# One transformer block with 32 experts on one core: a fixed TensorE order around the router, a split first gather, later norm vectors, and padded weight places

## The chip, the core and the metric

The kernel runs on one core of a Trainium2 chip. The core has five engines with a queue each: TensorE (PE; its weight loads are shown apart as PEld), VectorE (DVE), ScalarE (ACT), GpSimd (POOL) and SyncE (SP), which here issues nearly all DMAs. Each queue is worked in order, and engines wait for each other by semaphores. 16 DMA engines move data between HBM and SBUF; TensorE writes to PSUM. The metric is the device time of one execution in microseconds (us); the median of the runs is compared.

## The reference, cut to what matters

256 tokens of width 1024 go through one block. The mixer (three kinds of attention and state space branches) ends in a projection; its sum with the residual is normalised; a router picks 4 of 32 experts per token; the experts' outputs are added with softmaxed gates; a second normalisation follows.

```python
mix = merged @ w_o
h = layer_norm(ALPHA * h + mix, ln1_g, ln1_b)
logits = h @ w_router + b_router                    # [256, 32]
top_val, top_idx = top_k(logits, 4); gate = softmax(top_val)
for e in range(32):                                  # tokens that chose e
    g, lin = split(x_e @ w_gate_up[e] + b_gate_up[e])    # w_gate_up[e]: 1024 x 2048
    act = min(g, 7) * sigmoid(1.702 * min(g, 7)) * (clip(lin, -7, 7) + 1)
    ffn[tokens of e] += gate * (act @ w_down[e] + b_down[e])
out = layer_norm(ALPHA * h + ffn, ln2_g, ln2_b)
```

All of it is in float32; the experts' weights are 32 x 12 MiB.

## The kernel before

**Tiles.** The 256 tokens are two tiles t of 128 rows; `h` holds both. The width 1024 is 8 pieces k of 128 for products, and two halves n of 512 for PSUM banks.

**The weight stream.** `chunk` (L74) issues one DMA of 1 MiB, 128 rows of 8 KB, on SP's queue into a slot of 8 KB a partition. There are 24 such slots under four tags (13 u, 3 w, 4 s, 4 z); a pattern hands them out in turn, and other big tiles take their turns in the same slots: the halves of `w_o`, `xT1` (the transposed tokens for the router), `r` (what is left of `h` after a rounding to bf16) and `l1s` (the first norm's scale and shift, spread over the partitions). An expert has 12 chunks, 8 of `w_gate_up` and 4 of `w_down`, loaded in the order gate_up of expert e, then down of expert e - 1. SP's queue is in order: a chunk that waits until its slot has been read holds up all behind it. Around the router, the chunks that are due wait in turn for project (L208), the router's logits, expert 0's first reads (`pl` L1094), and the slot of `r`. The slots lie behind the small tiles of pool `cp`, from byte 7136 of each partition on, which is 480 past a multiple of 512 and 224 past one of 256.

**Around the router.** `project(t, n, k)` adds the product with piece k of `w_o` to a PSUM bank by three matmuls (L206 to L208). `half(t, n)` adds that bank to `h` (DVE L924), transposes four blocks of it (PE L927), copies them to `xT1` (ACT L928), takes statistics, and multiplies by the router's weights (PE L933, the logits). `route(t)` ends the norm without its scale and shift (`rs`, `nmr` on DVE, then ACT L948 on `h`), marks the four greatest logits (`selb`, DVE L953), counts the rank of each token in its expert's list (PE L956 and L957; called rank here) and writes `posm`, the places (DVE L959).

**Expert 0.** `sel` picks the expert's row of the biases (GpSimd). One-hot matrices `oh` (DVE L1046) gather the tokens' rows of both tiles from `h` by 16 matmuls of float32 (PE L1060), 8 pieces by 2 tiles, accumulating in PSUM; DVE and ACT put the norm's scale and shift on and write `xT`. `then`, which is `residual` for expert 0, splits `h` into three bf16 terms for later gathers, then spreads the norm's vectors by `spread` (PE L144, four groups of 4 matmuls into tile `pc`), copies them to `l1s` (ACT L1004) and applies them to `acc`, which is `h` (DVE L1008 and L1009). `pw` transposes the places with gates for the later scatter (L1083). The bias matmuls come next, then `up` (L1094): for each k a pair of matmuls to `pg` and one to `pl`, each pair reading one chunk. Experts from 1 on gather from the bf16 terms.

**What sets the order.** The program is traced into a scheduler that simulates a timeline and orders each engine's queue by it; `tc.issue_after(x)` fixes that what is traced inside comes after x. Tiles' readers and writers get their semaphores from the same pass.

Of the kernel before, what the change touches and what calls it, by code (L numbers as in the profile page):

```python
# [56 lines left out]
def block_kernel(ctx: ExitStack, tc: tile.TileContext, a: dict, out: bass.AP):  # L57
# [44 lines left out]
    G.memset(one, 1.0)  # L102
    lg = [cp.tile([128, NE + 4], F32, name=f"lg{t}") for t in range(NT)]
# [78 lines left out]
    with ExitStack() as fx:  # L182
# [735 lines left out]
        raw, stats = [], [f2.tile([128, 2, 6], F32, tag="bs", name="bs") for t in range(NT)]  # L918

        def half(t, n):  # L920


            zh = h[:, t, n * 512:(n + 1) * 512]
            V.scalar_tensor_tensor(zh, pz[t][n], 0.5 / ALPHA, zh, op0=OP.mult, op1=OP.add)  # L924
            p = bank("mm" if t else "tr")
            for k in range(4):
                PE.transpose(p[:, k * 128:(k + 1) * 128], zh[:, k * 128:(k + 1) * 128], ident)  # L927
            S.activation(xT1[:, 4 * n:4 * n + 4, t * 128:(t + 1) * 128], p.rearrange("p (k c) -> p k c", k=4), AF.Copy)  # L928
            V.bn_stats(stats[t][:, n, :], zh)
            if n == 0:  # L930
                raw.append(bank("sc", 3))
            for k in range(4 * n, 4 * n + 4):
                PE.matmul(raw[t][:, :NE], xT1[:, k, t * 128:(t + 1) * 128], wr[:, k, :], start=k == 0, stop=k == KT - 1)  # L933

        def route(t):
# [6 lines left out]
            lgt = lg[t][:, :NE]  # L942
            V.scalar_tensor_tensor(lgt, swr, nmr[:, 0:1], raw[t][:, :NE], op0=OP.mult, op1=OP.add)
            V.scalar_tensor_tensor(lgt, lgt, rs, brt, op0=OP.mult, op1=OP.add)
            tt(nmr[:, 1:2], nmr[:, 0:1], rs, OP.mult)
            for n in range(2):
                zh = h[:, t, n * 512:(n + 1) * 512]
                S.activation(zh, zh, AF.Identity, scale=rs, bias=nmr[:, 1:2])  # L948

# [3 lines left out]
            V.tensor_scalar(selb[:, t, :], mark[:, :NE], 3e38, None, op0=OP.is_equal)  # L953
            p = bank("mm" if t else "tr")
            for tp in range(t):
                PE.matmul(p[:, :NE], onesb, selb[:, tp, :], start=tp == 0, stop=False)  # L956
            PE.matmul(p[:, :NE], before, selb[:, t, :], start=t == 0, stop=True)  # L957

            V.scalar_tensor_tensor(posm[:, t, :], selb[:, t, :], -1e6, p[:, :NE], op0=OP.mult, op1=OP.add)  # L959

        for k in range(2, KT):
            project(1, 0, k)
        for n in range(2):
            half(0, n)
        route(0)
        for k in range(2, 5):
            project(1, 1, k)
        half(1, 0)
        for k in range(5, KT):
            project(1, 1, k)  # L970
        half(1, 1)
        route(1)
# [16 lines left out]
    def residual(x):  # L989
# [43 lines left out]
    def expert(mp, pm, gu, dn, pick_e, pos_e, gate_e, slots, then=None, last=None, after=None, first=False):  # L1033
# [6 lines left out]
        if first:  # L1040
            oh = mp.tile([128, 512], F32, tag="aT", name="oh", bufs=1)[:, :NT * CAP].rearrange("p (t c) -> p t c", t=NT)
        else:
            oh = mp.tile([128, NT, CAP], BF, tag="oh", name="oh")
        og = mp.tile([128, NT, 128], F32, tag="og", name="og", bufs=1)
        for t in range(NT):
            end = V.tensor_scalar(oh[:, t, :], slots[:, :CAP], pos_e(t), None, op0=OP.is_equal)  # L1046
        if first:
            with tc.issue_after(end.ins):
                gates(mp)
        for t in range(NT):  # L1050
            V.tensor_scalar(og[:, t, :], slots, pos_e(t), gate_e(t), op0=OP.is_equal, op1=OP.mult)
        xT = mp.tile([128, KT, CAP], F32, tag="xT", name="xT")
        xg = pm.tile([128, KT, CAP], F32, tag="xg", name="xg", bufs=1)
        if first:

            xg1 = pm.tile([128, 512], F32, tag="pc", name="xg", bufs=2)[:, :256].rearrange("p (k c) -> p k c", k=4)
            for k in range(KT):
                o = xg[:, k, :] if k < 4 else xg1[:, k - 4, :]
                for t in range(NT):
                    after = PE.matmul(o, h[:, t, k * 128:(k + 1) * 128], oh[:, t, :], start=t == 0, stop=t == 1)  # L1060
            wide_l = lambda i: lc[:, i, 0:4, None].to_broadcast([128, 4, CAP])
            tt(xT[:, 0:4], xg[:, 0:4], wide_l(0), OP.mult)
            tt(xT[:, 0:4], xT[:, 0:4], wide_l(1), OP.add)
            for k in range(4, KT):
                S.activation(xT[:, k, :], xg1[:, k - 4, :], AF.Identity, scale=lc[:, 0, k:k + 1], bias=lc[:, 1, k:k + 1])
        else:
            for k in range(KT):
                n = 0
                for b in range(3):
                    for t in range(NT):  # L1070
                        PE.matmul(xg[:, k, :], hb[t][b][:, k * 128:(k + 1) * 128], oh[:, t, :], start=n == 0,  # L1071
                                  stop=n == 5)
                        n += 1
            tt(xT, xg, lc[:, 0, :, None].to_broadcast([128, KT, CAP]), OP.mult)
            gg(xT, xT, lc[:, 1, :, None].to_broadcast([128, KT, CAP]), OP.add)

        if then:
            with tc.issue_after(after.ins):
                then(xT[:, KT - 1, 0:1])

        pw = pm.tile([128, 512], F32, tag="pt", name="pw", bufs=1)
        for t in range(NT):
            PE.transpose(pw[:, t * 128:(t + 1) * 128], og[:, t, :], ident)  # L1083
        ohT = mp.tile([128, 256], F32R, tag="ohT", name="ohT", bufs=3)
        gs = mp.tile([128, 1], F32, tag="gs", name="gs", bufs=3)
        V.tensor_scalar(ohT, pw[:, :256], 0.0, None, op0=OP.is_gt)
        V.tensor_reduce(gs, pw[:, :256], axis=AX.X, op=OP.max)

# [9 lines left out]
        with tc.issue_after(after.ins) if after else ExitStack():  # L1098
            up(pg, 0, sel, bias, True, False)
            up(pl, DFF, sel, bias, True, False)  # L1100
        for k in range(KT):
# [70 lines left out]
    for e in range(NE):  # L1172
# [3 lines left out]
        if e == NE - 1:  # L1176
            weights(e, KT, 12)
            l2 = big("l2", [128, 2, 2, 512])
            for i in range(4):
# [5 lines left out]
                      residual if e == 0 else further_blocks if e == 1 else None, last, after, e == 0)  # L1185
# [161 lines left out]
```

## Time and profile before

| | |
|---|---|
| median of 3 runs | 1289.65 us (1288.69 to 1295.11) |
| the profiled execution's own time | 1292.44 us |
| its span | 1290.7 us |
| mean granted TensorE clock | 0.985 |
| busy: PE, PEld, DVE, ACT, POOL | 1225.6, 623.2, 579.6, 285.6, 55.7 us |
| moved by DMA | 451.95 MB |

The span is the time from the first to the last instruction of the profiled execution. The page cuts it into 40 slices of 32.3 us. [...] In the views, `<-` in an operation stands between what is written and what is read; behind a row's duration, a bracket tells how long the engine had been idle and what ended it. Where rows are grouped (x8), the duration is that of the group.

### The profile page before, as it was taken

The page shows a single profiled execution, that of the slowest core. Times are in us where ns is not written, and L with a number is a line of the kernel's source. Part 1 is how long each engine was busy: PE and PEld are TensorE (multiplying, and loading weights), DVE is VectorE, ACT ScalarE, POOL GpSimd, SP SyncE. Part 2 cuts the span into 40 slices and gives each one's busy share as a digit, 9 for nine tenths or more (in the row PEclk, how much of TensorE's full clock was granted, in tenths as well). Part 3 has the DMA queues.
Part 4 walks back from the last instruction along what each step waited for, and adds up shares of the span by engine and source line. Part 5 has one row for each costly group of instructions (what it writes and reads, how often), then busy time and mean ns, then how long its engine had stood idle before and what let it go on. Part 6 is the DMA issues. An engine that isn't in the chain of part 4 may idle for free. (4 is left out here: it accounts for less than half of the span.)

```text
span 1290.7 us, 17685 instructions
## 1 busy us (share of the span) xinstructions
PE 1225.6 (95%) x7261; PEld 623.2 (48%) x7262; DVE 579.6 (45%) x1170; ACT 285.6 (22%) x514; POOL 55.7 (4%) x104
## 2 busy tenths in 40 slices
PE   7999999999999999999999999999999989999994
PEld 6657898789634434444444443333333333333331
DVE  6699975667633423334333343333333333333225
ACT  4245659863311000000100000010000000000111
POOL 1000000000000000000000000000000000000000
PEclk9999989999799999999999999999999999999998
DMA  7344447357799999999999999999999999999993
GB/s 273 105 137 183 169 147 224 133 189 305 284 420 418 420 419 419 419 420 419 419 418 420 418 419 419 420 420 418 420 419 419 420 418 420 420 419 420 419 419 120
DMA packets 65333, 451.95 MB, mean 350 GB/s; under 512 B 8896, under 2 KB 9056, under 8 KB 11360
## 3 DMA queue, kind: packets, MB, share of 16 engines
q1 hardware_dynamic: 64960, 450.26, 86.2%
q8 instruction: 58, 0.95, 0.3%
q10 hardware_dynamic: 288, 0.52, 0.1%
q14 instruction: 27, 0.22, 0.0%
HBM read 449.70 MB, written 1.05 MB: 349 GB/s over the span
## 5 line engine op out<-in xcount | busy, mean ns | idle before, releaser
L1094 PE MATMUL pg<-w,xT 128*64 128x512 f32 x1024 | 292.8, 608 | 13.0 <-DMA w<-in_w_gate_up 11.4
L1094 PE MATMUL pl<-w,xT 128*64 128x512 f32 x1024 | 285.8, 593 | 0.0
L1141 PE MATMUL py<-w,aT 128*64 128x512 f32 x1024 | 241.7, 599 | 18.5 <-DMA w<-in_w_down 17.7
L78 DVE TENSOR_TENSOR h<-h,pc 128x512 f32<-128x512 f32 x128 | 82.2, 684 | 294.9 <-PE pc L1156 294.9
L1094 PEld LDWEIGHTS pl<-w,xT 128*64 128x64 f32 x1024 | 95.0, 137 | 127.9 <-issue 104.7
L1141 PEld LDWEIGHTS py<-w,aT 128*64 128x64 f32 x1024 | 69.5, 136 | 158.7 <-issue 95.1
L1114 ACT ACTIVATE sg<-gc 128x512 f32<-128x512 f32 x32 | 20.1, 630 | 564.4 <-DVE gc L1113 564.4
L1094 PEld LDWEIGHTS pg<-w,xT 128*64 128x64 f32 x1024 | 74.7, 136 | 132.0 <-DMA w<-in_w_gate_up 67.5
L1148 DVE SCALAR_TENSOR_TENSOR ys<-py,gs,ys 128x512 fp32r<-128x512 f32 x64 | 48.0, 751 | 169.4 <-ACT ys L1147 166.3
L1147 ACT ACTIVATE ys<-py,gs 128x512 fp32r<-128x512 f32 x64 | 44.0, 688 | 253.5 <-PE py L1141 238.0
L1156 PE MATMUL pc<-ys,ohT 128*128 128x512 f32 x256 | 77.0, 422 | 0.9 <-DVE h L78 0.8
L1156 PEld LDWEIGHTS pc<-ys,ohT 128*128 128x128 f32 x256 | 42.9, 188 | 57.9 <-issue 50.7
L194 DVE TENSOR_TENSOR hl<-w,hl 128x1024 fp32r<-128x1024 f32 x48 | 58.2, 1221 | 14.9 <-ACT hl L193 14.7
L81 POOL TENSOR_TENSOR xT<-xT,lc 128x512 f32<-128x512 f32 x31 | 39.8, 1284 | 525.6 <-DVE xT L78 525.6
L208 PE MATMUL mm<-hTh,hl 128*128 128x256 f32 x192 | 57.1, 298 | 2.0 <-DVE hl L194 2.0
L1071 PEld LDWEIGHTS <-hb 128*128 128x128 bf16 x1240 | 45.0, 98 | 27.5 <-issue 26.7
L206 PE MATMUL mm<-hTh,hl 128*128 128x256 f32 x192 | 57.4, 299 | 0.0
L207 PE MATMUL mm<-hTl,hl 128*128 128x256 f32 x192 | 56.4, 294 | 0.0
L193 ACT ACTIVATE hl<-w 128x1024 fp32r<-128x1024 f32 x48 | 50.0, 1054 | 26.6 <-DMA w<-in_w_g 13.9
L1113 DVE TENSOR_SCALAR gc<-pg 128x512 f32<-128x512 f32 x32 | 22.1, 692 | 71.1 <-PE pg L1094 71.1
L1071 PE MATMUL xg<-oh,hb 128*128 128x64 bf16 x1240 | 49.7, 193 | 0.0
L1071 PE MATMUL xg<-oh,bias 128*128 128x64 bf16 x248 | 44.2, 193 | 0.0
(390 smaller groups left out, 1454.0 us busy)
## 6 DMA issues: line engine op xcount, KB each, us to landing
w<-in_w_gate_up SPq DMA_DIRECT2D x256, 1024.0 KB, 19.9
w<-in_w_down SPq DMA_DIRECT2D x128, 1024.0 KB, 19.9
w<-in_w_g SPq DMA_DIRECT2D x12, 1024.0 KB, 4.9
w<-in_w_s_glu SPq DMA_DIRECT2D x4, 1024.0 KB
w<-in_w_o SPq DMA_DIRECT2D x4, 1024.0 KB, 4.8
w<-in_w_memk SPq DMA_DIRECT2D x2, 1024.0 KB, 10.2
w<-in_w_u SPq DMA_DIRECT2D x2, 1024.0 KB, 8.6
w<-in_w_memv SPq DMA_DIRECT2D x2, 1024.0 KB, 5.2
```

What stands on the lines that cost most here:

```text
L78: V.tensor_tensor(o, x, y, op=op)
L193: S.activation(hi, src, AF.Copy)
L194: (eng or V).tensor_tensor(lo, src, hi.bitcast(F32), op=OP.subtract)
L206: PE.matmul(o, lhsT(0), rhs(0), start=start, stop=False)
L207: PE.matmul(o, lhsT(0), rhs(1), start=False, stop=False)
L208: PE.matmul(o, lhsT(1), rhs(0), start=False, stop=stop)
L1071: PE.matmul(xg[:, k, :], hb[t][b][:, k * 128:(k + 1) * 128], oh[:, t, :], start=n == 0, stop=n == 5)
L1094: m = PE.matmul(p_[hf * 64:(hf + 1) * 64, :], lhsT, w[:, o + hf * 512:o + (hf + 1) * 512], start=start, stop=stop)
L1141: end = PE.matmul(py[j * 64:(j + 1) * 64, :], a4[:, k // 4, k % 4 + j, :], dn(k + j, hf), start=k + j == 1, stop=k == 6)
L1147: S.activation(y2[:, 0], py, AF.Copy, scale=gs)
L1148: V.scalar_tensor_tensor(y2[:, 1], py, gs, y2[:, 0].bitcast(F32), op0=OP.mult, op1=OP.subtract)
L1156: PE.matmul(pc, ohT[:, t * 128:(t + 1) * 128], ys[hf][:, i], start=i == 0, stop=i == 1)
```

## The change

Five things are changed.

1. TensorE's order around the router is written out: a function `step` puts each piece after the piece before by `issue_after`. `half` and `route` are split into `residual_half`, `turn` (transposes), `logits`, `norm`, `four` and `rank`.
2. The first expert's gather is split by tile. Tile 0's 8 pieces are gathered as soon as tile 0's places are known, into a bank of their own (`xg0`), and ACT writes them with scale and shift to `x0`. Tile 1's 8 pieces follow later, and DVE scales them and adds `x0`. Expert 0's bias matmuls come before the gather of tile 1, the places' transposes after its second k.
3. `l1s` and its ACT copies are gone; `start_sum` lets DVE read the spread vectors from PSUM, and it runs in expert 1 behind k = 3 and k = 5.
4. `l1s` no longer takes a slot from the weights.
5. A pad of 32 bytes a partition in pool `cp` moves the slots from byte 7136 to 7168, a multiple of 512.

```diff
@@ pool cp
+    cp.tile([128, 8], F32, name="pad")
...
@@ around the router
+        def step(f, *args):
+            with tc.issue_after(done[0].ins) if done[0] else ExitStack():
+                done[0] = f(*args) or done[0]
...
-        for k in range(2, KT):
-            project(1, 0, k)
-        for n in range(2):
-            half(0, n)
-        route(0)
-        for k in range(2, 5):
-            project(1, 1, k)
-        half(1, 0)
-        for k in range(5, KT):
-            project(1, 1, k)
-        half(1, 1)
-        route(1)
+        some(0, range(2, KT - 1))
+        done[0] = project(1, 0, KT - 1)
+        for n in range(2):
+            residual_half(0, n)
+            step(turn, 0, n)
+        residual_half(1, 0)
+        step(some, 1, range(2, 5))
+        step(turn, 1, 0)
+        raw = [bank("sc", 3) for t in range(NT)]
+        step(logits, 0)
+        n0 = norm(0)
+        four(0, *n0)
+        step(some, 1, range(5, KT))
+        residual_half(1, 1)
+        step(rank, 0)
+
+        oh0 = fp.tile([128, CAP], F32)
+        V.tensor_scalar(oh0, slot[:, :CAP], posm[:, 0, 0:1], None, op0=OP.is_equal)
+        step(turn, 1, 1)
+        n1 = norm(1)
+        xg0 = bank("av", 1).rearrange("p (k c) -> p k c", c=CAP)
+        step(gather, xg0, h[:, 0, :], oh0, range(0, 2))
+        step(logits, 1)
+        four(1, *n1)
+        step(gather, xg0, h[:, 0, :], oh0, range(2, KT))
+        x0 = hb2.bitcast(F32).rearrange("p (k c) -> p k c", c=CAP)
+        for k in range(KT):
+            S.activation(x0[:, k, :], xg0[:, k, :], AF.Identity, scale=lc[:, 0, k:k + 1], bias=lc[:, 1, k:k + 1])
+        step(rank, 1)
+        ranked = done[0]
@@ residual, for expert 0
-        l1s = big("l1s", [128, 4, 512], **at("l1s"))
-        for i in range(4):
-            S.activation(l1s[:, i], spread(gb1, i, pm.tile([128, 512], F32, tag="pc", name="pc", bufs=2)), AF.Copy)
-        for i in range(2):
-            for t in range(NT):
-                at_ = acc[:, t, i * 512:(i + 1) * 512]
-                V.scalar_tensor_tensor(at_, at_, ALPHA, l1s[:, i], op0=OP.mult, op1=OP.mult)
-                V.scalar_tensor_tensor(at_, l1s[:, 2 + i], ALPHA, at_, op0=OP.mult, op1=OP.add)
+    def start_sum(i):
+
+        g_, b_ = (spread(gb1, 2 * j + i, pm.tile([128, 512], F32, tag="pc", name="pc", bufs=2)) for j in range(2))
+        for t in range(NT):
+            at_ = acc[:, t, i * 512:(i + 1) * 512]
+            V.scalar_tensor_tensor(at_, at_, ALPHA, g_, op0=OP.mult, op1=OP.mult)
+            V.scalar_tensor_tensor(at_, b_, ALPHA, at_, op0=OP.mult, op1=OP.add)
@@ expert
+        if first:
+
+            oh = mp.tile([128, 512], F32, tag="aT", name="oh", bufs=1)[:, :CAP]
+            end = V.tensor_scalar(oh, slots[:, :CAP], pos_e(1), None, op0=OP.is_equal)
+            with tc.issue_after(end.ins):
+                gates(mp)
+            xg1 = pm.tile([128, 512], F32, tag="pc", name="xg", bufs=2).rearrange("p (k c) -> p k c", c=CAP)
+
+            with tc.issue_after(ranked.ins):
+                end = biases()
+            with tc.issue_after(end.ins):
+                for k in range(KT):
+                    PE.matmul((xg, xg1)[k // 4][:, k, :], h[:, 1, k * 128:(k + 1) * 128], oh, start=True, stop=True)
+            for i, p_ in enumerate((xg, xg1)):
+                sl = slice(4 * i, 4 * i + 4)
+                tt(xT[:, sl], p_[:, sl], wide_l(0)[:, sl], OP.mult)
+                tt(xT[:, sl], xT[:, sl], x0[:, sl], OP.add)
...
+            if first and k == 1:
+                with tc.issue_after(end.ins):
+                    places()
...
-                      residual if e == 0 else further_blocks if e == 1 else None, last, after, e == 0)
+                      residual if e == 0 else further_blocks if e == 1 else None,
+                      start_sum if e == 1 else last, after, e == 0)
```

TensorE's queue between project and the router, before. `av` is the bank of tile 1's second half, `hl` the pieces of `w_o` (`hl_2873` is k = 5, `hl_2902` k = 6, `hl_2905` k = 7), `tr` and `mm` the banks of the transposes of tile 0 and 1, `sc` the logits.

```order
L207 MATMUL av_2691<-hl_2873,mgTh_2672 128x512
L208 MATMUL av_2691<-hl_2873,mgTl_2673 128x512
L206 MATMUL av_2691<-hl_2902,mgTh_2672 128x512
L927 MATMUL tr_2942<-ident_61,h_180 128x128 x4
L927 MATMUL tr_2955<-ident_61,h_180 128x128 x4
L207 MATMUL av_2691<-hl_2902,mgTh_2672 128x512
L208 MATMUL av_2691<-hl_2902,mgTl_2673 128x512
L206 MATMUL av_2691<-hl_2905,mgTh_2672 128x512
L207 MATMUL av_2691<-hl_2905,mgTh_2672 128x512
L208 MATMUL av_2691<-hl_2905,mgTl_2673 128x512
L927 MATMUL mm_3005<-ident_61,h_180 128x128 x4
L933 MATMUL sc_2949<-s_w_router_421,xT1_2867 128x32 x8
```

And the same stretch after; here `hl_2848`, `hl_2851` and `hl_2871` are k = 2 to 4, `hl_2874` is k = 5.

```order
L209 MATMUL av_2692<-hl_2848,mgTl_2674 128x512
L207 MATMUL av_2692<-hl_2851,mgTh_2673 128x512
L208 MATMUL av_2692<-hl_2851,mgTh_2673 128x512
L209 MATMUL av_2692<-hl_2851,mgTl_2674 128x512
L207 MATMUL av_2692<-hl_2871,mgTh_2673 128x512
L208 MATMUL av_2692<-hl_2871,mgTh_2673 128x512
L209 MATMUL av_2692<-hl_2871,mgTl_2674 128x512
L938 MATMUL mm_2969<-ident_61,h_181 128x128 x4
L945 MATMUL sc_2975<-s_w_router_422,xT1_2868 128x32 x8
L207 MATMUL av_2692<-hl_2874,mgTh_2673 128x512
L208 MATMUL av_2692<-hl_2874,mgTh_2673 128x512
L209 MATMUL av_2692<-hl_2874,mgTl_2674 128x512
```

Before, k = 5 of project stands ahead of all transposes and logits. After, the transposes of tile 0 (in the two rows ahead of these), those of tile 1's first half and tile 0's logits stand ahead of k = 5.

TensorE's queue at the start of expert 0, before. `xg` are the gathered rows, `pc` the spread vectors, `pw` the places, `w_1621` the first chunk.

```order
L1060 MATMUL xg_3106<-oh_3084,h_180 128x64
L1060 MATMUL xg_3107<-oh_3084,h_180 128x64
L1060 MATMUL xg_3106<-oh_3084,h_180 128x64 x7
L1060 MATMUL xg_3107<-oh_3084,h_180 128x64 x7
L144 MATMUL pc_3142<-gbin_ln1_g_2676,ident_61 128x128 x4
L1083 MATMUL pw_3174<-ident_61,og_3085 128x128 x2
L1094 LDWEIGHTS sel_3082
L1094 MATMUL pg_3181<-bias_441,sel_3082 64x512
L1094 LDWEIGHTS sel_3082
L1094 MATMUL pg_3181<-bias_441,sel_3082 64x512
L1094 LDWEIGHTS sel_3082
L1094 MATMUL pl_3182<-bias_441,sel_3082 64x512
```

And after, from the end of rank(1) on; `w_1622` is the same chunk.

```order
L976 LDWEIGHTS before_2687
L976 MATMUL mm_3084<-selb_2921,before_2687 128x32
L1097 LDWEIGHTS sel_3102
L1097 MATMUL pg_3107<-bias_442,sel_3102 64x512
L1097 LDWEIGHTS sel_3102
L1097 MATMUL pg_3107<-bias_442,sel_3102 64x512
L1097 LDWEIGHTS sel_3102
L1097 MATMUL pl_3108<-bias_442,sel_3102 64x512
L1097 LDWEIGHTS sel_3102
L1097 MATMUL pl_3108<-bias_442,sel_3102 64x512
L1117 MATMUL xg_3106<-oh_3109,h_181 128x64 x4
L1117 MATMUL xg_3126<-oh_3109,h_181 128x64 x4
```

The gather is half as long here, the bias matmuls stand ahead of it, and the spread and the places are no longer between gather and up.

SP's queue of weight chunks, with the waits, before: the first rows are those that wait for project, the row with `Activation_49` waits for the logits (`xT1`'s slot), the next for expert 0's first k, the one with `DVE_49` for `r`'s slot.

```order
L74 DMA w<-in_w_gate_up 128x2048 [waits DMAHW7_49,PE_49]
L74 DMA w<-in_w_gate_up 128x2048 [waits PE_49]
L74 DMA w<-in_w_gate_up 128x2048 [waits DMAHW1_49,PE_49]
L74 DMA w<-in_w_gate_up 128x2048 [waits DMAHW2_49]
L74 DMA w<-in_w_down 128x2048 [waits DMAHW3_49]
L74 DMA w<-in_w_down 128x2048 [waits DMAHW4_49,PE_49,Activation_49]
L74 DMA w<-in_w_gate_up 128x2048 [waits DMAHW5_49,PE_49]
L74 DMA w<-in_w_down 128x2048 [waits DMAHW6_49,DVE_49]
```

And after.

```order
L74 DMA w<-in_w_gate_up 128x2048 [waits DMAHW7_49,PE_49]
L74 DMA w<-in_w_gate_up 128x2048 [waits PE_49]
L74 DMA w<-in_w_gate_up 128x2048 [waits DMAHW1_49,PE_49]
L74 DMA w<-in_w_gate_up 128x2048 [waits DMAHW2_49]
L74 DMA w<-in_w_down 128x2048 [waits DMAHW3_49]
L74 DMA w<-in_w_down 128x2048 [waits DMAHW4_49]
L74 DMA w<-in_w_down 128x2048 [waits DMAHW5_49,PE_49,Activation_49]
L74 DMA w<-in_w_gate_up 128x2048 [waits DMAHW6_49,PE_49]
L74 DMA w<-in_w_gate_up 128x2048 [waits DMAHW7_49,PE_49]
L74 DMA w<-in_w_down 128x2048 [waits DMAHW0_49,DVE_49]
```

One chunk of `w_down` more, which waits for an earlier DMA alone, stands ahead of the row that waits for expert 0's first k, and the chunk behind that waits for its second k.

## Rows read from the trace of the kernel before

**Rows 1.** The page's slices: what the DMA engines moved, GB/s in 40 equal slices.

```profile
GB/s 273 105 137 183 169 147 224 133 189 305 284 420 418 420 419 419 419 420 419 419 418 420 418 419 419 420 420 418 420 419 419 420 418 420 420 419 420 419 419 120
```

**Rows 2.** Long window: us; busy PE, PEld, DVE, ACT, POOL; PEclk, DMA share, GB/s.

```profile
600.00:800.00 200.00, 198.12 (x1186) 85.86 (x1184) 70.87 (x125) 18.73 (x29) 11.14 (x14) 1.00 1.01 419
```

**Rows 3.** Waits of the whole span: total us, times, longest us.

```profile
PEld pg L1094 <- DMA w<-in_w_gate_up: 67.5, 69, 2.6
```

**Rows 4.** Windows of 2 us around the router; columns as in group 2.

```profile
324.00:326.00 2.00, 2.00 (x13) 1.67 (x12) 1.86 (x11) 0.00 (x0) 0.00 (x0) 1.00 0.36 147
326.00:328.00 2.00, 2.00 (x15) 1.74 (x14) 0.80 (x4) 1.85 (x4) 0.00 (x0) 1.00 0.70 193
...
334.00:336.00 2.00, 1.61 (x8) 1.64 (x8) 2.00 (x17) 0.53 (x2) 0.63 (x3) 0.50 0.99 418
...
342.00:344.00 2.00, 2.00 (x9) 1.44 (x9) 0.15 (x1) 1.78 (x4) 0.00 (x0) 0.50 0.23 94
344.00:346.00 2.00, 2.00 (x9) 0.87 (x10) 1.89 (x5) 1.67 (x3) 0.00 (x0) 0.50 0.00 0
346.00:348.00 2.00, 2.00 (x8) 0.51 (x6) 2.00 (x3) 1.38 (x2) 0.00 (x0) 0.75 0.00 0
348.00:350.00 2.00, 2.00 (x10) 0.82 (x7) 2.00 (x4) 0.73 (x1) 0.00 (x0) 1.00 0.43 115
...
352.00:354.00 2.00, 2.00 (x15) 1.02 (x15) 1.21 (x3) 0.60 (x1) 0.00 (x0) 1.00 0.81 270
```

**Rows 5.** SP's queue: issues (start us, us), and its waits in 323:333 and 345:357.

```profile
325.47 3.30 SPq L74 DMA_DIRECT2D w<-in_w_gate_up  x4
...
347.86 0.33 SPq L74 DMA_DIRECT2D w<-in_w_gate_up  x1
351.14 0.33 SPq L74 DMA_DIRECT2D w<-in_w_down  x1
...
SPq L74 <- PE av L208: 12.8, 2, 10.9
...
SPq L74 <- PE pl L1094: 19.2, 3, 15.3
```

**Rows 6.** TensorE's timeline, router to first up: start us, us, idle before.

```profile
325.51 1.03 PE L927 MATMUL tr<-ident,h 128*128 128x128 f32 x8
326.30 0.48 PE L207 MATMUL av<-hl,mgTh 128*128 128x512 f32 x1
...
327.54 0.60 PE L927 MATMUL mm<-ident,h 128*128 128x128 f32 x4
327.97 1.87 PE L933 MATMUL sc<-s_w_router,xT 128*128 128x32 f32 x16
329.68 0.63 PE L927 MATMUL mm<-ident,h 128*128 128x128 f32 x4
...
333.44 0.18 PE L957 MATMUL mm<-selb,before 128*128 128x32 bf16 x1 [1.32 <-DVE selb L953]
334.39 7.06 PE L1060 MATMUL xg<-oh,h 128*128 128x64 f32 x32 [0.76 <-DVE oh L1046]
341.38 2.07 PE L144 MATMUL pc<-gbin_ln_g,ident 16*128 16x128 f32 x8
...
344.00 0.64 PE L1094 MATMUL pg<-bias,sel 128*64 128x512 bf16 x2
...
344.86 1.92 PE L1094 MATMUL pg<-w,xT 128*64 128x512 f32 x4
```

**Rows 7.** ScalarE's and DVE's timeline: scaling of gathered rows, a norm vector's use.

```profile
341.49 1.29 ACT L1065 ACTIVATE xT<-xg,lc 128x64 f32<-128x64 f32 x4 [6.37 <-PE xg L1060]
...
351.28 1.29 DVE L1008 SCALAR_TENSOR_TENSOR h<-h,l1s 128x512 f32<-128x512 f32 x2 [0.16 <-ACT l1s L1004]
```

**Rows 8.** DMA packets, MB, share of 16 engines, in 15.17:15.27 and 21.94:21.97.

```profile
q1 hardware_dynamic: 92, 0.00, 58.6%
...
q1 hardware_dynamic: 13, 0.00, 29.4%
```

More of the change, by code (lines that the diff above doesn't have):

```diff
@@ L1038, in expert @@
         G.tensor_copy(sel, pick_e.to_broadcast([128, CAP]))
[L1040 to L1043, printed above, removed]
         og = mp.tile([128, NT, 128], F32, tag="og", name="og", bufs=1)
[L1045 to L1049, printed above, removed]
@@ L1050, in expert @@
-        for t in range(NT):
-            V.tensor_scalar(og[:, t, :], slots, pos_e(t), gate_e(t), op0=OP.is_equal, op1=OP.mult)
         xT = mp.tile([128, KT, CAP], F32, tag="xT", name="xT")
         xg = pm.tile([128, KT, CAP], F32, tag="xg", name="xg", bufs=1)
[L1054 to L1087, printed above, removed]
+        wide_l = lambda i: lc[:, i, :, None].to_broadcast([128, KT, CAP])
@@ L1096, in up, with biases @@
             return m
-        with tc.issue_after(after.ins) if after else ExitStack():
+        def biases():
             up(pg, 0, sel, bias, True, False)
-            up(pl, DFF, sel, bias, True, False)
+            return up(pl, DFF, sel, bias, True, False)
+        if first:
[7 more added lines that the diff above has]
+            with tc.issue_after(end.ins):
+                for k in range(KT):
+                    PE.matmul((xg, xg1)[k // 4][:, k, :], h[:, 1, k * 128:(k + 1) * 128], oh, start=True, stop=True)
[3 more added lines that the diff above has]
+                tt(xT[:, sl], xT[:, sl], x0[:, sl], OP.add)
+        else:
+            oh = mp.tile([128, NT, CAP], BF, tag="oh", name="oh")
+            for t in range(NT):
+                V.tensor_scalar(oh[:, t, :], slots[:, :CAP], pos_e(t), None, op0=OP.is_equal)
+            for k in range(KT):
+                n = 0
+                for b in range(3):
+                    for t in range(NT):
+                        PE.matmul(xg[:, k, :], hb[t][b][:, k * 128:(k + 1) * 128], oh[:, t, :], start=n == 0, stop=n == 5)
+                        n += 1
+            tt(xT, xg, wide_l(0), OP.mult)
+            gg(xT, xT, wide_l(1), OP.add)
@@ new lines, in expert, with places @@
+        for t in range(NT):
+            V.tensor_scalar(og[:, t, :], slots, pos_e(t), gate_e(t), op0=OP.is_equal, op1=OP.mult)
+        if then:
+            then(xT[:, KT - 1, 0:1])
+        pw = pm.tile([128, 512], F32, tag="pt", name="pw", bufs=1)
+        ohT = mp.tile([128, 256], F32R, tag="ohT", name="ohT", bufs=3)
+        gs = mp.tile([128, 1], F32, tag="gs", name="gs", bufs=3)
+        def places():
+            for t in range(NT):
+                PE.transpose(pw[:, t * 128:(t + 1) * 128], og[:, t, :], ident)
+            V.tensor_scalar(ohT, pw[:, :256], 0.0, None, op0=OP.is_gt)
+            V.tensor_reduce(gs, pw[:, :256], axis=AX.X, op=OP.max)
@@ L1101, in expert @@
+        if not first:
+            places()
+        if not first:
+            with tc.issue_after(after.ins) if after else ExitStack():
+                biases()
         for k in range(KT):
```

47 lines of the change are left out of this document (32 added, 15 removed).

## Prediction

> **What bounds the kernel now.** I read the page's slices first: from about 350 us to 1258 us every slice moves 418 to 420 GB/s [rows 1], and a long window agrees, 419 GB/s at a DMA share of 1.01 [rows 2]. At 419 GB/s a chunk of 1 MiB takes 2.50 us, so an expert's 12 chunks take 30.0 us, and 32 experts 961 us. TensorE is nearly as busy (198.12 of 200 us [rows 2]); what it waits for by name is the weight stream [rows 3]. There is no hole in that stream after 354 us, so nothing that an engine does later can move the end, unless it opens one. What can be won is the time that the DMA engines lose before 354 us, and in the last stage before that, the router, they lose some [rows 4]. By the GB/s against 419: 324:326 moved 147, so the stream stopped at 324.70; 326:328 moved 193, so it went on at 327.08 (2.4 us lost); 342:344 moved 94 and 344:348 nothing, so it stopped at 342.45, and 348:350 moved 115, so it went on at 349.45 (7.0 us); 352:354 moved 270 (0.7 us).
>
> The sync engine's queue tells why. One chunk was issued at 325.47, after a wait of 10.9 us for project (L208), and 349.45 belongs to the one issued at 347.86, after a wait of 15.3 us for `pl` L1094: expert 0's first read of a weight slot [rows 5]. From issue to flow it is 1.6 us both times (327.08 - 325.47, 349.45 - 347.86), and 351.14 + 1.6 = 352.74 fits the third hole: the first of the two late chunks had run from 349.45 to 351.95, and from there to 352.74 is 0.8 us against the 0.7 seen. So three numbers decide: when project lets the first chunk go, how many chunks stand ready behind it, and when expert 0 has read its first slot.
>
> **The change part by part.** *The order around the router.* The matmul that lets the 325.47 chunk go is the last of `project(1, 1, 5)`. Ahead of it TensorE now does the 8 transposes of tile 0 (by the starts in [rows 6] 325.51 to 326.30, where project goes on: 0.79 us), the 4 transposes of tile 1's first half (327.54 to 327.97, 0.43 us) and the 8 logits instructions of tile 0 (327.97 to the next group at 329.68, 1.71 us). Sum 2.93 us: the stream goes on at 327.08 + 2.9 = 330.0, and the first hole grows from 2.4 to 5.3 us. This is the price, and nothing covers it, since the queue is empty there.
>
> *One more chunk ready.* `l1s` is gone, so its slot stays with the weights: before the first chunk that waits for expert 0's read, 7 chunks can now be issued instead of 6 (the order of the sync engine shows the added row). 330.0 + 7 x 2.50 = 347.5, and with the 0.3 us by which six chunks from 327.08 overran (342.45 instead of 342.08) the stream runs dry at 347.8 instead of 342.45. The eighth chunk started at 352.74 before; it now starts at 347.8 or 1.6 us after expert 0's first read, X, whichever is later.
>
> *When X comes.* Before, X was 347.86 by the chain rank(1) at 333.44, 32 passes of the gather in 7.06 us at half clock (granted 0.50 in 334:336, 0.75 in 346:348 [rows 4]), spreads 2.07, places and biases, and the first up [rows 6]. Now: project ends 0.43 + 1.71 us later, at 329.8 instead of 327.7 (the transposes of tile 0 were ahead of its end before too). Then come, one after the other, the DVE step on the last half of `h` and its copy to `xT1` (0.65 us each, as a 512-wide step in [rows 7]), 0.43 us of transposes and 1.71 of logits: 333.3, with an estimate of 0.9 for the hand-overs between engines 334.2, against 333.44 - 1.32 = 332.1 before; two gather instructions lie in those waits. The 1.32 us that TensorE then idled ahead of rank(1) now hold the other 6 gather instructions of tile 0: 12 passes of 7.06 / 32 = 0.22 us at half clock, 2.65 us, so to 336.9. Then ScalarE turns these 8 blocks into `x0`: nearest row 1.29 us for 4 [rows 7], so 2.6 us, to 339.5; the bias instructions wait for that, because they share the PSUM bank, and take 0.86 us (344.00 to 344.86), to 340.4; DVE's and GpSimd's steps for `posm`, `oh` and `sel` lie beside it. The gather of tile 1 is 16 passes, 3.5 us, to 343.9; the spreads are no longer there and the places come after the second k. The first up took 3.0 us (344.86 to 347.86): X = 346.9, with 0.4 us for its wait for `xT` 347.3. [...] I take 347.3, since narrow matmuls come at the same place as in the rows where the clock was 0.50. TensorE is then 1 us ahead of before in expert 0, and later 4 us, as three more spread groups leave.
>
> *The sum.* The eighth chunk starts at 347.3 + 1.6 = 348.9 instead of 352.74: 3.8 us sooner. Bounds: 4.9 us with X early, 1.1 us with X = 350. Chunk 10, which takes `r`'s slot, was let go at 351.14 [rows 5]; its chain is moved by less than a chunk and it is needed at 353.9. Behind it each chunk has TensorE's lead. The profiled execution, 1292.44 us with a span of 1290.7, would come to 1288.7; the median of the runs, 1289.65, less 3.7, is **1286.0 us**, -0.3%.
>
> *Norm's vectors read from PSUM later.* Four spread groups (half of 2.07 us each at full clock [rows 6], 4.1 us) and eight vector steps (1.29 us for two [rows 7], 5.2 us) move to expert 1 behind its k = 3 and 5, and four ScalarE copies vanish. I cost this at nothing, since the stream is the bound there and TensorE got the same groups out of expert 0; its cover is the lead of the slots. If that is gone, it is the third rival.
>
> *Places at multiples of 512.* 32 bytes of padding move the weight slots from byte 7136, 224 past a multiple of 256, to 7168. The trace has no big rows at such a place. An 8 KB row takes 2.50 x 16 / 128 = 0.313 us. Small rows bound it: 92 rows of 64 bytes to places 0 and 64 past such a multiple kept 16 engines busy for 58.6% of 0.10 us, 10.2 ns a row; 13 rows of 64 bytes, as the order of issue has it those for a place 224 past one, 29.4% of 0.03 us, 10.9 ns [rows 8]. A row that crosses the boundary costs no more than one that doesn't (0.7 ns of edge effect), so I take 0. The other end is one such piece saved from each 8 KB row, 10.9 of 313 ns or 3.5%, and a small loss can't be excluded either (1 ns, 0.3%, 3 us).
>
> [...]
>
> **Rivals.**
> 1. *The whole hole closes.* For it: fewer narrow passes stand in a row now, and project's wide ones lie among them, so the clock may fall later or not at all. Against: 0.50 held for 13 us of busy TensorE [rows 4, 6]. [...]
> 2. *Rows that start on a boundary are shorter.* It acts on the 915 us of stream behind 353 us: between 0 and 3.5%, middle 16 us on top of the forecast, **1270** (1254 to 1286). It needs only 0.3% of the row to count. [...] For it: only the small rows were seen; a saturated stream may behave otherwise.
> 3. *Expert 1 pays (slower).* Place: behind k = 3 and 5 of expert 1. 4.1 us on TensorE and 5.2 us of DVE ahead of that expert's activation, 9.3 us if none is hidden; against it stands the lead of some 4 us that expert 0 gains and the slots read but not yet refilled. It decides when more than 3.7 us of it reach the stream as a hole; at full price it is 1286.0 + 9.3 = **1295**, at half 1290.7, and 1300.5 if the vector steps, which now read PSUM, took twice as long.
> 4. *It doesn't do what it says.* The first hole's 2.9 us are certain, the gain is not: at X = 351.1, 3.8 us past my estimate, the two cancel: **1289.7**. [...]
>
> **How the numbers follow.** Forecast 0.52, rival 1 0.13, rival 2 0.17, rival 3 0.10, rival 4 0.08. About 0.5% (6.4 us) is what a measurement can tell from no change. The forecast, rivals 1 and 4 and the cheaper half of rival 3 lie within it: 0.78. Rival 2 lies nearly wholly beyond (0.16), the dearer half of rival 3 reaches past the other side (0.04). One of the three runs before lay 5.5 us over the median, so a few hundredths of the middle go to either side: faster 0.20, same 0.72, slower 0.08. The range reaches into rival 2 to 1276 (it leaves out some 0.12 below) and into rival 3 to 1293 (some 0.06 above); the likeliest case's own is 1284.5 to 1289.
>
> **What would show it.** In the profile after: the first chunk behind project issued near 328.4, a first hole of 5.3 us, seven chunks to 347.8, `pl` letting the next go at 347.3, and a hole under 2 us there; the clock's row tells the forecast from rival 1. A rate over 421 GB/s in the long stretch is rival 2. A hole between 375 and 410 us is rival 3. Wrong would be another hole later than 354 us, or a stream that doesn't end about as much sooner as the eighth chunk starts.

## The result and the profile after

The changed kernel takes 1274.46 us (median of 4, 1273.15 to 1275.26) beside 1292.38 us for the kernel before on the same chip: a ratio of 0.9861 (95% interval 0.9825 to 0.9896), 17.9 us faster. Measured once more later, unedited (run e9 below), it is 0.9854 (0.9833 to 0.9875). The forecast was 1286.0 us and -0.3%; the time lies below its range, and the size of the change is four to five times what I forecast. The sign of the router's part was right; the bulk came from what I had put at nothing.

The page's slices after (GB/s, as [rows 1]):

```profile
GB/s 273 109 126 191 150 156 218 130 171 299 327 414 425 427 426 426 426 426 426 426 427 427 426 427 427 426 426 426 427 427 426 427 426 427 426 427 427 425 426 120
```

From the thirteenth slice on it reads 425 to 427 where [rows 1] has 418 to 420. The long window says the same (columns as in [rows 2]):

```profile
600.00:800.00 200.00, 200.00 (x1242) 89.33 (x1239) 73.23 (x128) 18.68 (x29) 12.50 (x15) 1.00 1.01 426
```

426 against 419 GB/s, at the same DMA share. TensorE is now busy in all of this window, but the stream still has no gap, and by the waits of the whole span TensorE's weight loads still stand and wait for the stream (total us, times, longest us), so the stream still sets the time:

```profile
PEld pg L1097 <- DMA w<-in_w_gate_up: 53.3, 61, 1.5
```

A chunk of 1 MiB takes 2.46 us instead of 2.50. Over the 915 us behind the router that is 915 x (1 - 419 / 426) = 15.0 us of the 17.9.

The 2 us windows around the router (columns as in [rows 4]):

```profile
324.00:326.00 2.00, 2.00 (x11) 1.63 (x10) 1.90 (x11) 1.09 (x2) 0.00 (x0) 1.00 0.65 274
326.00:328.00 2.00, 2.00 (x20) 1.95 (x18) 0.76 (x5) 1.32 (x3) 0.00 (x0) 1.00 0.01 4
328.00:330.00 2.00, 2.00 (x12) 1.69 (x12) 1.13 (x6) 0.68 (x1) 0.00 (x0) 1.00 0.00 0
330.00:332.00 2.00, 1.21 (x8) 0.60 (x6) 1.44 (x4) 0.00 (x1) 0.00 (x0) 1.00 0.88 283
...
334.00:336.00 2.00, 2.00 (x11) 2.00 (x11) 0.84 (x5) 0.36 (x1) 0.00 (x0) 0.50 0.93 360
...
346.00:348.00 2.00, 2.00 (x8) 0.55 (x6) 0.75 (x3) 1.76 (x2) 0.00 (x0) 0.61 0.98 410
348.00:350.00 2.00, 2.00 (x11) 0.58 (x8) 2.00 (x3) 1.67 (x3) 0.00 (x0) 1.00 0.82 193
350.00:352.00 2.00, 2.00 (x12) 0.69 (x13) 2.00 (x2) 1.98 (x2) 0.00 (x0) 1.00 0.87 369
352.00:354.00 2.00, 2.00 (x12) 0.70 (x10) 1.31 (x5) 0.17 (x1) 0.00 (x0) 1.00 0.80 234
354.00:356.00 2.00, 2.00 (x12) 0.72 (x10) 0.00 (x0) 0.00 (x0) 0.00 (x0) 1.00 1.03 430
```

By the same reading as of [rows 4], now against 426: the stream stopped at 325.29 and went on at 330.67 (5.4 us; 2.4 before), stopped again at about 348.9 and went on at 350.3 (1.4 us; 7.0 before), and lost 0.9 us in 352:354 (0.7 before). The sync engine's queue (start us, us) and its waits in 323:333 and 345:360:

```profile
329.16 2.50 SPq L74 DMA_DIRECT2D w<-in_w_gate_up  x4
331.71 3.93 SPq L74 DMA_DIRECT2D w<-in_w_down  x3
348.24 2.04 SPq L74 DMA_DIRECT2D w<-in_w_gate_up  x2
352.16 0.33 SPq L74 DMA_DIRECT2D w<-in_w_down  x1
...
SPq L74 <- PE av L209: 14.1, 1, 14.1
...
SPq L74 <- PE pl L1097: 17.2, 5, 12.5
```

329.16 for [rows 5]'s 325.47, and 348.24 for its 347.86. Those clocks start at the span's start; the last issue of a `w_o` chunk lies at 302.56 us before and at 303.11 after, so 0.55 us has to be taken off the rows of after to compare. TensorE's timeline after (as [rows 6]):

```profile
335.06 2.80 PE L983 MATMUL av<-oh,h 128*128 128x64 f32 x12
337.65 0.23 PE L975 MATMUL mm<-selb,onesb 128*128 128x32 bf16 x1
337.73 0.19 PE L976 MATMUL mm<-selb,before 128*128 128x32 bf16 x1
340.43 0.64 PE L1097 MATMUL pg<-bias,sel 128*64 128x512 bf16 x2 [2.51 <-ACT hb L1018]
340.81 0.68 PE L1097 MATMUL pl<-bias,sel 128*64 128x512 bf16 x2
341.42 3.68 PE L1117 MATMUL xg<-oh,h 128*128 128x64 f32 x16
345.03 1.98 PE L1097 MATMUL pg<-w,xT 128*64 128x512 f32 x4
346.79 1.41 PE L1097 MATMUL pl<-w,xT 128*64 128x512 f32 x4
```

### The profile page after: what moved, and what is told of

Same layout as the page of the kernel before. It is cut to its first block, busy times and chain, and to the rows that moved or that the text cites. A ratio compares the mean times of both kernels' runs of the same rounds, so it can differ in the third digit from the quotient of the medians.

```text
span 1273.5 us, 17688 instructions
## 1 busy us (share of the span) xinstructions
PE 1218.1 (96%) x7261; PEld 627.0 (49%) x7262; DVE 580.9 (46%) x1172; ACT 284.7 (22%) x514; POOL 55.4 (4%) x104
## 5 line engine op out<-in xcount | busy, mean ns | idle before, releaser
L1097 PE MATMUL pl<-w,xT 128*64 128x512 f32 x1024 | 281.9, 593 | 0.0
## 6 DMA issues: line engine op xcount, KB each, us to landing
w<-in_w_memk SPq DMA_DIRECT2D x2, 1024.0 KB, 10.2
```

Source lines behind the costliest of these rows:

```text
L1097: m = PE.matmul(p_[hf * 64:(hf + 1) * 64, :], lhsT, w[:, o + hf * 512:o + (hf + 1) * 512], start=start, stop=stop)
```

## Experiments

Each kernel is compared with the kernel before, run beside it on the same chip. The order of each engine is that of the kernel named, unless the diff moves it.

**e1: the padding alone.**

```diff
 (the kernel before)
     G.memset(one, 1.0)
+    cp.tile([128, 8], F32, name="pad")
```

> The kernel before with the 32 bytes of padding alone: the weight slots start at byte 7168, every instruction stays in its order. Theory 1 (the place of the rows in the partition sets the rate of the saturated stream): 426 GB/s instead of 419 in the long windows, 915 us of stream shorter by 1.7%, so 15 to 16 us faster than before, and the holes around the router as before (2.4, 7.0 and 0.7 us). Theory 2 (the rate rose for another reason: the new order, or the chip and its state): 419 GB/s as before and the time of before within 2 us.

1275.89 us against 1293.4: 0.9871 (0.9841 to 0.9901). The long window of e1:

```profile
600.00:800.00 200.00, 200.00 (x1242) 89.47 (x1240) 73.20 (x128) 18.68 (x29) 12.48 (x15) 1.00 1.01 426
```

Theory 1 holds and theory 2 falls: with the old order untouched, the same 426 GB/s. The hole ahead of the first waiting chunk is still there in e1 (342:344 moved 12 GB/s, 344:346 none, 346:348 16).

**e2: the change without the padding.**

```diff
 (the changed kernel)
-    cp.tile([128, 8], F32, name="pad")
```

> The changed kernel without its 32 bytes of padding: slots at byte 7136 again, the order of every engine that of the changed kernel. Theory 1: 419 GB/s, so 15 to 16 us slower than the changed kernel, and faster than before by what the router's new order is worth, 2 to 4 us. Theory 2: 426 GB/s and the time of the changed kernel.

1289.29 us against 1293.4: 0.9966 (0.9952 to 0.998), 4.4 us faster by the ratio, between 2.6 and 6.2.

```profile
600.00:800.00 200.00, 198.53 (x1193) 86.14 (x1190) 72.10 (x126) 18.73 (x29) 12.28 (x15) 1.00 1.01 419
```

419 GB/s again. This is the whole of the router's and the norm vectors' part, and 3.7 us is what the sum had for it. The two parts come to 16.7 and 4.4 us by their ratios, 21.1 together; both at once gave 18.0 (and 18.9 in e9), so within the intervals they add up, or a little is lost. The profiles show what can be lost. Take as the stream's own clock the time, from the last `w_o` issue on, until 45 MiB in rows of 8 KB have ended in the packet records: 125.70 us before, 124.72 in e1, 121.66 in e2, 121.02 in e3 (below) and 122.04 in the changed kernel. So the router's part is 4.0 us in e2 against before and 3.7 in e3 against e1, but 2.7 in the changed kernel against e1. The stretch of half clock behind the router lasted 10.2 us in e2 and e3 and 13.7 in the changed kernel, before and e1.

**e3, e4 and e8: which place.** The tile named is allocated in a pool behind the slots instead of ahead of them, so that the slots move down by its size; the order stays. While the weights stream, the other SBUF pools in use are those allocated from the other side (`side="right"` in the kernel), so only the slots and some small tiles of `cp` move.

```diff
 (the changed kernel; e3: posm, 256 bytes; e4: lc, 64 bytes; e8: stack, 128 bytes)
     slots = ctx.enter_context(tc.tile_pool(name="slots", bufs=1))
+    cp2 = ctx.enter_context(tc.tile_pool(name="cp2", bufs=1))
...
-    posm = cp.tile([128, NT, NE], F32)
+    posm = cp2.tile([128, NT, NE], F32)
```

> The changed kernel with the slots from byte 6912 on, a multiple of 256 but not of 512 (posm lies behind the slots instead of ahead of them), same order. If a multiple of 256 is what counts: 426 GB/s and the time of the changed kernel within 1 us. If 512 counts: 419 GB/s and 15 us slower than it.

> The changed kernel with the slots from byte 7104 on, a multiple of 64 that is 192 past a multiple of 256 (lc lies behind the slots), same order. If only multiples of 256 or 512 count: 419 GB/s, 15 us slower than the changed kernel. If a multiple of 64 is enough, because before was at 32 past one: 426 GB/s and the same time.

> The changed kernel with the weight slots from byte 7040 on, 128 past a multiple of 256 (stack lies behind the slots), same order. Slots 224 past one cost 1.7% of the stream's rate (419 of 426 GB/s), 192 past one 1.2% (421). If the price falls with the distance from the boundary below: 423 to 424 GB/s, 6 to 9 us slower than the changed kernel. If any place off a multiple of 256 costs the same: 419 to 421 GB/s, 12 to 15 us slower. If a multiple of 128 is free: 426 GB/s.

e3 takes 1274.03 us, 0.9843 (0.9817 to 0.9869); e4 1286.27, 0.9937 (0.9913 to 0.9961); e8 1284.14, 0.9933 (0.9912 to 0.9955). The long window of e3:

```profile
600.00:800.00 200.00, 200.00 (x1242) 89.39 (x1240) 73.19 (x128) 18.68 (x29) 12.50 (x15) 1.00 1.01 427
```

of e4:

```profile
600.00:800.00 200.00, 199.38 (x1236) 88.02 (x1234) 73.24 (x128) 18.71 (x29) 12.49 (x15) 1.00 1.01 421
```

and of e8:

```profile
600.00:800.00 200.00, 200.00 (x1240) 89.33 (x1238) 73.33 (x129) 18.70 (x29) 12.51 (x15) 1.00 1.01 421
```

A multiple of 256 is enough, 512 is not needed: e3, with its slots from byte 6912 on, runs at 427 GB/s, the changed kernel, from 7168 on, at 426. 192 and 128 past one run at 421, 224 past one at 419, so neither "64 is enough" nor "128 is free" holds, and the price does not fall in proportion to the distance between 192 and 128. Against 426.5 the losses are 1.8% at 224 and 1.3% at 192 and at 128. Neither rate expected of e4 (419 or 426) came; e8 has a rate of its second case and, 9.7 to 10.8 us behind the changed kernel by the medians, a time between its first two.

**e5: project first.** Is it the first hole or expert 0's first read that sets the router's part?

```diff
 (the changed kernel; logits takes the k's to do as a second argument)
-        for n in range(2):
-            residual_half(0, n)
-            step(turn, 0, n)
-        residual_half(1, 0)
-        step(some, 1, range(2, 5))
+        for n in range(2):
+            residual_half(0, n)
+        residual_half(1, 0)
+        step(some, 1, range(2, 6))
+        step(turn, 0, 0)
+        step(turn, 0, 1)
+        step(some, 1, range(6, KT))
         step(turn, 1, 0)
...
         step(logits, 0)
         n0 = norm(0)
+        residual_half(1, 1)
         four(0, *n0)
-        step(some, 1, range(5, KT))
-        residual_half(1, 1)
+        step(turn, 1, 1)
+        n1 = norm(1)
+        step(logits, 1, range(0, 4))
         step(rank, 0)
...
-        step(turn, 1, 1)
-        n1 = norm(1)
...
-        step(gather, xg0, h[:, 0, :], oh0, range(0, 2))
-        step(logits, 1)
+        step(logits, 1, range(4, KT))
         four(1, *n1)
-        step(gather, xg0, h[:, 0, :], oh0, range(2, KT))
+        step(gather, xg0, h[:, 0, :], oh0, range(0, KT))
```

> The changed kernel with project(1, 1, 2..7) ahead of tile 1's transposes and of both logits again, so that the stream's first hole is 2.4 us instead of 5.3; the gather of tile 0 runs in one piece behind the logits of tile 1. If the stream's first hole sets the time: 2.9 us faster than the changed kernel. If the eighth chunk, let go by expert 0's first read X, sets it (it started at X + 1.6 to 1.9 and not when the seven ready chunks were through): only what X moves, about 1 us faster, and the hole ahead of the eighth chunk grows from 1.3 to 3 us.

1269.74 us, 0.983 (0.9812 to 0.9847): by the medians 3.6 to 4.7 us faster than the changed kernel (1273.31 to 1274.46). The two were not run beside each other and the ratios' intervals overlap, but each run of e5 (up to 1270.73) lies below each of the changed kernel (from 1272.22). By the stream's own clock it is 3.2 us: 45 MiB in 118.85 us, 122.04 in the changed kernel. Its windows:

```profile
322.00:324.00 2.00, 2.00 (x14) 1.71 (x13) 1.80 (x11) 0.06 (x1) 0.00 (x0) 1.00 0.41 172
324.00:326.00 2.00, 2.00 (x15) 1.70 (x13) 0.57 (x3) 2.00 (x4) 0.00 (x0) 1.00 0.68 205
...
342.00:344.00 2.00, 2.00 (x12) 0.58 (x8) 2.00 (x2) 1.75 (x2) 0.00 (x0) 0.90 0.31 107
344.00:346.00 2.00, 2.00 (x12) 0.69 (x10) 2.00 (x5) 1.90 (x3) 0.00 (x0) 1.00 0.78 319
```

The first hole is 2.2 us by 322:326 (172 and 205 of 426), and the one ahead of the eighth chunk 342:346 is 2.0 us (107 and 319), about as much as the changed kernel's 1.4 and 0.9 together. So the gain is as large as the 3.2 us taken from the first hole, but only because both ends moved: the chunks behind project came 3.1 us sooner, and X came sooner by 2.9 us on the clock that starts at the last `w_o` issue (42.2 us behind it, 45.1 in the changed kernel), of which I had expected 1. TensorE's timeline shows two differences that can have moved X: the DVE step on tile 1's last half now lies beside the logits of tile 0, so that the logits of tile 1 end right behind those, and the granted clock stayed at 0.50 for 10.2 us instead of 13.7. The second can be sized: e2, e3 and e4 have the changed kernel's order, 10.2 us at 0.50, and X at 43.5 to 43.6. So 1.5 to 1.6 us of the 2.9 go with the shorter stretch, and 1.3 to 1.4 with the order. Against e3, which has the same rate, e5's stream gains 2.2 us (118.85 against 121.02), not 3.2. That e5, e7 and e11 all have 10.2 us may come from the order; no run shows it.

**e6 and e7: the bias matmuls behind the gather; both.**

```diff
 (the changed kernel: e6; with e5's order and rank(1) behind three of tile 0's gathers: e7)
             with tc.issue_after(ranked.ins):
-                end = biases()
-            with tc.issue_after(end.ins):
                 for k in range(KT):
-                    PE.matmul((xg, xg1)[k // 4][:, k, :], ...)
+                    end = PE.matmul((xg, xg1)[k // 4][:, k, :], ...)
+            with tc.issue_after(end.ins):
+                biases()
```

> The changed kernel with expert 0's bias matmuls behind the gather of tile 1 instead of ahead of it, so that TensorE does not idle 2.5 us for x0. First hole as in the changed kernel, 5.3 us. X 1.5 to 1.8 us sooner than its 348.2, the hole ahead of the eighth chunk nearly closed, 1.4 us faster. If X does not set it: no change.

> Both edits, and rank(1) after three of tile 0's eight gathers: first hole 2.4 us and X at about 344.5. Both causes together: the eighth chunk starts 3.5 to 4 us sooner than in the changed kernel, 3.5 us faster, about 1271. If a hole at 352 to 354 that the issue times do not explain stays, 0.9 us of the loss stay with it.

e6 takes 1272.1 us, 0.9846 (0.9828 to 0.9864), e7 1271.48, 0.9846 (0.9827 to 0.9866). e6's median is 1.2 to 2.4 us below the changed kernel's, e7's 1.7 above e5's: neither difference is clear of the intervals. In e6's profile X did come 1.7 us sooner than in the changed kernel's, as expected, but not by the edit: e3, with the changed kernel's order and the same 10.2 us at 0.50, has it at the same place. The last `w_o` issue and X of e3, then of e6, 43.5 us apart in both:

```profile
303.72 0.38 SPq L75 DMA_DIRECT2D w<-in_w_o  x1
347.22 2.04 SPq L75 DMA_DIRECT2D w<-in_w_gate_up  x2
...
304.80 0.38 SPq L74 DMA_DIRECT2D w<-in_w_o  x1
348.28 2.04 SPq L74 DMA_DIRECT2D w<-in_w_gate_up  x2
```

The row that tells is the gather's, first in e6, then in e7:

```profile
340.68 3.68 PE L1115 MATMUL xg<-oh,h 128*128 128x64 f32 x16 [2.65 <-ACT hb L1018]
```

```profile
336.39 3.68 PE L1117 MATMUL xg<-oh,h 128*128 128x64 f32 x16 [2.56 <-ACT hb L1021]
```

The 2.5 us of idle did not go away: it moved from the bias matmuls to the gather. Both expectations named the wrong cause, the bank, and where their times were met (e7's 1271) it was not by it. The bias's tile and the gather's are two banks, so the one that `x0` reads can be at most one of them. What both have in common is that they are the first to write a PSUM tile of the experts' pool, which in the kernel's text follows the pool that served the mixer and the router, and `x0` is the last to read from that one. That the new pool waits for the whole old one fits e5, e6 and e7, but no run changes the pool alone. In e7 `x0` also started 1.7 us later than in e5 (31.6 and 33.3 us behind the last `w_o` issue), as tile 0's gather was cut in two.

**e9 and e10: the changed kernel again, and with `l1s` in its slot.**

```diff
 (e10: the changed kernel; e9: no edit)
     def residual(x):
...
+        l1s = big("l1s", [128, 4, 512], **at("l1s"))
+        V.memset(l1s[:, 0, 0:1], 0.0)
```

> The changed kernel once more, unedited, beside the next two on one chip, so that they are compared with it directly: 0.986 of the kernel before, 1274 us. In its profile X and the hole ahead of the eighth chunk may differ by 1 to 2 us from the first profile, if the length of the low-clock stretch (13.7 us there, 10.2 us in three of the edited kernels) is a matter of the run and not of the code.

> The changed kernel with the tile l1s allocated again in its slot (one column is written, nothing reads it), so that 6 chunks instead of 7 stand ready ahead of the one that waits for expert 0's first read; all else as in the changed kernel. If the extra chunk carries the gain of the router's part, as the sum has it: the stream runs dry one chunk sooner, at about 346 instead of 348.7, the hole ahead of the first waiting chunk grows by 2.5 us, 2.5 us slower than the changed kernel. If X alone decides and the extra chunk is only shifted: the same time.

e9 takes 1273.31 us, e10 1273.91, 0.9852 (0.9835 to 0.9869): 0.6 us apart, no difference that can be measured. The windows of e10 show that the mechanism is there all the same:

```profile
346.00:348.00 2.00, 2.00 (x8) 0.63 (x6) 0.75 (x3) 1.56 (x2) 0.00 (x0) 0.50 0.11 37
348.00:350.00 2.00, 2.00 (x12) 0.50 (x8) 2.00 (x4) 1.69 (x2) 0.00 (x0) 0.91 0.28 33
350.00:352.00 2.00, 2.00 (x10) 0.69 (x10) 2.00 (x2) 1.95 (x2) 0.00 (x0) 1.00 0.75 299
```

346 to 352 us moved 37, 33 and 299 GB/s, 4.3 us lost where the changed kernel lost 2.3 (348 to 354). By the stream's own clock e10 took 123.54 us and e9 121.92: 1.6 us, not 2.5. The 0.9 us hole behind the eighth chunk is not there in e10, and 0.9 us is what lacks to 2.5. X and the low clock's length were the same in e9 as in the first profile; e2, with the same order, had 10.2 us of it, so the run does matter, but not between these two.

**e11: `x0` on DVE.**

```diff
 (e5's kernel)
-        for k in range(KT):
-            S.activation(x0[:, k, :], xg0[:, k, :], AF.Identity, scale=lc[:, 0, k:k + 1], bias=lc[:, 1, k:k + 1])
         step(rank, 1)
+        wide0 = lambda i: lc[:, i, :, None].to_broadcast([128, KT, CAP])
+        tt(x0, xg0, wide0(0), OP.mult)
+        tt(x0, x0, wide0(1), OP.add)
```

> Project first as in e5, and x0 made by two wide DVE steps instead of eight on ScalarE, because the first matmul into a PSUM tile behind the router waits until x0 has read its bank (2.5 us of idle in e5, e6 and e7 alike). The idle falls to 1.0 us or less, X 1.3 to 1.5 us sooner than e5's, the hole ahead of the eighth chunk 2.0 to about 0.7 us: 1.2 us faster than e5, 1268.5, and 6 us faster than the changed kernel. If the idle has another cause, the time of e5.

1269.14 us, 0.9826 (0.9805 to 0.9847), the fastest of the kernels here and 0.6 us from e5: not to be told apart. TensorE's row in e5, then in e11:

```profile
334.70 0.64 PE L1097 MATMUL pg<-bias,sel 128*64 128x512 bf16 x2 [2.52 <-ACT hb L1018]
...
333.12 0.64 PE L1098 MATMUL pg<-bias,sel 128*64 128x512 bf16 x2 [1.56 <-POOL sel L1087]
```

The idle fell from 2.52 us in e5 to 1.56, and what ends it now is GpSimd's `sel`; so the idle hung on `x0`, and another wait stands 1 us ahead of its end. X came 41.5 us behind the last `w_o` issue, 0.7 us sooner than in e5 and not the 1.3 to 1.5 expected.

## Why the prediction was wrong, step by step

**What bounds the kernel: right.** The stream set the time before and after, and what the holes gave back showed at the end.

**The places: the step that failed.** The prediction took 0, between 0 and 3.5%, for the place at which a row of 8 KB starts; it measures 1.7 to 1.8% of the stream, some 15 us. Rival 2, with its middle of 16 us, named the place and nearly the size, and was given 0.17. The argument from [rows 8] was that a small row past a boundary costs no more than one on it, and that is true of the small rows: 64 bytes take 11 ns in both traces. It was the wrong row to reason from, since a row alone is not a row in a full stream. The trace of before held the right ones, which I did not look for. Two windows of the kernel before, the first right behind the last hole, the second a little later (columns as in [rows 2]):

```profile
354.00:360.00 6.00, 6.00 (x32) 2.49 (x30) 0.92 (x3) 0.87 (x2) 0.00 (x0) 1.00 1.01 429
400.00:420.00 20.00, 19.55 (x125) 9.34 (x121) 6.35 (x10) 2.01 (x3) 0.00 (x0) 1.00 1.01 418
```

The same rows to the same places ran at 429 GB/s when the stream had just begun again, and at 418 when it had run for a while. The packet records of the trace say it sharper; of the rows of 8 KB that start in a stretch, the share that took 309 ns, and those that took longer:

```
                 309 ns   310 to 317   318 to 324
before  354-360   1.00       0.00         0.00
before  366-372   0.38       0.46         0.16
before  384-390   0.08       0.68         0.24
before  400-1200  0.07       0.70         0.23
e2      366-372   0.05       0.72         0.23
e8      360-366   1.00       0.00         0.00
e8      400-1200  0.28       0.49         0.23
e1      400-1200  1.00       0.00         0.00
```

So a misplaced row takes no longer by itself: 309 ns at either place. It does once the stream has run without a break for some 10 to 30 us, when 313 and 320 ns become the rule (in e8 for three rows in four). No run shows why; the engines that read the slots read them at the moved places too. What is shown is that the loss goes with the place (1.8, 1.3 and 1.3% at 224, 192 and 128 past a multiple of 256), is absent at multiples of 256, and takes time to build up (0.38 of the rows of before still took 309 ns in 366-372, 0.08 in 384-390).

**The first hole: right.** Forecast 5.3 us and a first issue near 328.4; measured 5.4 us and 329.16 - 0.55 = 328.6.

**X: right, for a reason that was half wrong, and with some luck.** Forecast 347.3, measured 348.24 - 0.55 = 347.7, by the pieces forecast: `x0`'s wait 2.51 us, gather 3.68, first up 3.2. The wait was laid to a shared bank; e6 and e7 show that it falls on the first instruction that writes a tile of the next PSUM pool, there the gather's (2.65 and 2.56 us of idle). The price was the same, but an edit made on the strength of that reason gained nothing. The closeness is partly luck: with the shorter stretch of half clock of e2 to e4 the same order had X 1.5 us sooner. The 0.9 us in that chain for the hand-overs between engines is my estimate, and no run shows it by itself; the chain that holds it was to end at 334.2, and the next group started at 335.06 - 0.55 = 334.5. Nor does any run show the bounds of the sum, an X early enough for a gain of 4.9 us and X = 350: X came between 41.5 (e11) and 45.1 us (changed kernel) behind the last `w_o` issue, 344.1 to 347.7 on the clock of before, with 10.2 to 13.7 us at 0.50 ahead of it, and in the changed kernel and e5 a hole of 1.4 and 2.0 us stayed.

**Seven chunks ready: right in kind, smaller in worth.** The stream was to run dry at 347.8 (the overrun of 342.45 over 342.08 is 0.37 us, so 347.9 rather); it did at 348.9 - 0.55 = 348.4. The eighth chunk started at 350.3 - 0.55 = 349.7 against 348.9; e10 values the seventh at 1.6 us of stream, not 2.5.

**The sum for the router: right.** 3.7 us forecast, 4.4 (2.6 to 6.2) measured in e2; by the stream's own clock 2.7 to 4.0, by the length of the half clock.

**Norm's vectors in expert 1: right.** There is no hole between 375 and 410 us, and rival 3 did not come (columns as in [rows 2]):

```profile
375.00:410.00 35.00, 35.00 (x199) 17.63 (x199) 13.78 (x24) 3.29 (x5) 1.28 (x2) 1.00 1.01 425
```

Rival 1 did not come either, since X kept a hole of 1.4 us open; rival 4 is refuted by e2.

**Still open:** the hole of 0.6 to 0.9 us one chunk behind the eighth (352:354 in the changed kernel), although its chunk was issued at 349.96, 2.6 us ahead of it; and why the low clock lasted 13.7 us in some profiles and 10.2 in others (the last section has what goes with it).

## What to carry to other kernels

When a transfer stream is the bound, compare its rate in the first microseconds behind a gap with its rate after a long run, and its row time with the shortest row time of the same size: a difference there can be a gain that no reordering gives (here 15 us). Put big tiles that DMAs write at multiples of 256 bytes of the partition (shown here for rows of 8 KB: 426 to 427 GB/s there, 419 to 421 at 128, 192 and 224 past one), and count what stands ahead of them in the pool. And where a wait is to be removed, change its cause in a run before building on it: here an idle of 2.5 to 2.65 us moved with the first instruction into a new PSUM pool and looked like a bank conflict.

## What the runs showed of the hardware that was not expected

- Rows of 8 KB written at 224, 192 or 128 bytes past a multiple of 256 of the partition ran at 419, 421 and 421 GB/s in the long stream, at a multiple of 256 at 426 to 427; in a fresh stream the single row takes 309 ns at 224 and at 128 past one too (before, 354-360, and e8, 360-366), and the longer times (313, 320 ns) come up only as the stream goes on without a break (of the rows of before 0.38 at 309 ns in 366-372, 0.08 in 384-390).
- The stretch of half clock behind the router (granted 0.50) differs between runs of one order of instructions: 13.7 us in the changed kernel, e8 and e9, 10.2 us in e2, e3 and e4. From the changed kernel to e2, X moved by 1.5 us (45.1 to 43.6 us behind the last `w_o` issue). In each of these profiles an earlier stretch at 0.50, near 180 us, had the other length: 10.2 us where this one had 13.7, and 13.7 where this one had 10.2. So the length goes with something that lies ahead of the router; its cause is open.
